# A hybrid attention and Hyena layer: bias tables assembled in DRAM, and the long convolutions without GpSimd

## The chip, the core and the metric

The kernel runs on one core of a Trainium2 chip. The metric is the device time of one execution in microseconds (us); lower is better. Below, PE is TensorE, DVE is VectorE, ACT is ScalarE, POOL is GpSimd and SP is SyncE, which here issues nearly all DMA transfers. "L841" is line 841 of the kernel before.

## What is computed

One layer over 1024 latent tokens (a grid of 16 rows by 64 columns) and 256 context tokens, model width 1024. After a modulated norm, one input projection feeds eight attention heads of 64 and a Hyena group of 512 channels. Both results are normed, put side by side and projected out; a gated ConvFFN (2816) follows. Cut to what the change touches:

```python
def _long_conv(u, k_f, bias):                      # FFT convolution, length 2L
    y = irfft(rfft(u, n=2*L) * k_f[None], n=2*L)[:, :L]
    return y + u * bias

def _hyena(hy, k_f, filt_bias):                    # two orders, one after the other
    x1, x2, v = jnp.split(hy, 3, axis=-1)
    z = x1 * _long_conv(v, k_f[:, 0], filt_bias[0])
    return x2 * _long_conv(z, k_f[:, 1], filt_bias[1])

def _neighbourhood_attention(q, k, v, k_ctx, v_ctx, rpb):
    # each latent query sees an 8 x 16 window of the grid (clipped at the edges) and all context keys
    bias = rpb[:, dr[:, None, :, None], dc[None, :, None, :]]
    s_loc = jnp.where(col_in, einsum(q, k_band) * scale + bias, NEG)    # NEG = -1e30
    s_ctx = einsum(q, k_ctx) * scale
    p = softmax(concatenate([s_loc, s_ctx]))
    ...
```

## The kernel before, in words

**Stage A** (to about 591 us): the norm, then 24 projections, each of 128 columns of the input weight over all 1280 tokens. A projection's weight arrives by one 512 KB DMA (`wr`, L606), is split into a high and a low part (`wh`, `wl`; three matmuls L116 to L118 replace one of full precision), with two buffers of each. The projections alternate between `qkv` and `hy_chunk`. `hy_chunk` (L652) applies the width-3 convolution on ACT and DVE into `cv` (two buffers), folds the result into the tile `fo` (POOL L663, L664, or ACT and DVE for one of three), transposes `fo` on PE and stores it to DRAM as `lxd` and `cxd`. **`fo` has one buffer.** Between the projections PE computes the implicit filters' spectra (matmuls into `psfA` and `psfB`), stored to DRAM as `Kd` and `Kc`. `rpb_frames` (L550) runs three times after the first group of projections. For each of three column variants it spreads the small bias table into frames, also in a tile with the tag `fo`, and stores them as `rpw` in DRAM (L558).

**Stage B** (about 437 to 915 us) has two strands. `chain(j)` (L770) computes the long convolutions, for four blocks of latent channels (j = 0 to 3) and once for the context (j = 4). Each call has two orders, here called *half-chains*, and each needs the one before it: forward DFT on PE (L802), twiddles (ACT L814 and L815, DVE L816), a butterfly over four residues (L823 to L828), the product with the filter's spectrum `K` (L841 to L844), an inverse butterfly (L849 to L854), twiddles (L858 to L860), inverse DFT on PE (L872), and a gate product (L877 to L885). The context's half-chains have no butterflies and no twiddles. The frequencies lie in two halves, h = 0 and 1; the butterflies and the product are written once for each half, dealt out between DVE and POOL. `K` has one buffer for each parity of j and comes in two loads of 512 KB, one for each half (L837). `attend(p_)` (L1001) handles a pair of heads, four times: scores (PE L1021), bias added and maximum taken on DVE (L1042), exponentials on ACT, transposes of the probabilities (PE L1065), products with the values (PE L979). Its bias comes in six tables `tb` of 128 x 736 numbers (two heads, three variants), which POOL fills once with NEG (L941); for each pair, 96 DMAs of 16 KB (L959) bring the rows of the frames into place.

**Stage C** (from about 915 us): group norms, output projection, ConvFFN, final norm.

The order of the work on each engine is fixed when the program is built, by a scheduler that runs the program through a model of the engines; `chain` is given high priority. On the chip each engine then runs its list strictly in order, and so does SP with its DMA issues; a DMA also waits for the one eight places ahead of it to be complete, because eight completion semaphores take turns.

The lines that the change and the prediction speak of:

Of the kernel before, what the change touches and what calls it, by code (L numbers as in the profile page):

```python
# [11 lines left out]
F32 = mybir.dt.float32  # L12
# [7 lines left out]
P = 128  # L20
# [3 lines left out]
LT = LL + LC  # L24
NH, DH = 8, 64
# [4 lines left out]
NEG = -1e30  # L30
# [44 lines left out]
HALF_ROWS = ((0, 11), (4, 12))  # L75
# [11 lines left out]
def _build(nc, tc, top, V, A, G, T, Q, I, O, dbg, upto):  # L87
# [458 lines left out]
    NROW = HALF_ROWS[0][1] + HALF_ROWS[1][1]  # L546
    HOFF = (0, HALF_ROWS[0][1] * 32)
    rpw = dr.tile([3, 16, NH, 4, 120], F32, name="rpw")

    def rpb_frames(t, var):  # L550
        f, g = t[:, 0:480], t[:, 512:992]
# [100 lines left out]
    def hy_chunk(which, j):  # L652

        cv = hyin((8, 0, 4)[which] + j)
        v = cv[:, 0:LL].rearrange("p (j r) -> p r j", r=4)
        lo, up = v[:, :, 0:128], v[:, :, 255:127:-1]
        clo, cup = cv[:, LL:LL + 128], cv[:, LL + 255:LL + 127:-1]
        fo = ip.tile([P, 2, 640], F32, tag="fo", name="fo", bufs=1)
        for i in range(2):
            d, dc = fo[:, i, 0:512].rearrange("p (r j) -> p r j", r=4), fo[:, i, 512:640]  # L660
            if which < 2:
                f = G.tensor_sub if i else G.tensor_add
                f(d, up, lo)  # L663
                f(dc, cup, clo)  # L664
            else:
                A.copy(d, up if i else lo)
                V.tensor_copy(dc, cup if i else clo)
        for i in range(2):
            ps = bk("tB")
            for r in range(4):  # L670
                T.transpose(ps[:, r * P:(r + 1) * P], fo[:, i, r * P:(r + 1) * P], ident)
            t = ip.tile([P, 512], F32, tag="st", name="st", bufs=2)
            A.copy(t, ps)
            Q.dma_start(out=lxd[j, which, :, i], in_=t)
        ps = bk("tB")
        for i in range(2):
            T.transpose(ps[:, i * P:(i + 1) * P], fo[:, i, 512:640], ident)
        t = ip.tile([P, 2, P], F32, tag="st", name="cx", bufs=2)
        A.copy(t, ps[:, 0:256].rearrange("p (i c) -> p i c", i=2))
        Q.dma_start(out=cxd[which, :, :, j * P:(j + 1) * P], in_=t)  # L680
# [56 lines left out]
    for j in range(4):  # L737
        for which in range(3):
            if j + which > 0:
                qkv(j, which)  # L740
            hy_chunk(which, j)
            if j + which == 0:

                t = ft([P, 512], "tm", bufs=2)
                e = "p a b -> p (a b)"
                Q.dma_start(out=t, in_=I["t_dft"].flatten().rearrange("(p x) -> p x", p=P))
                split(t, dft[0].rearrange(e), dft[1].rearrange(e))
                Q.dma_start(out=dlt, in_=I["t_delta"])
                Q.dma_start(out=nt, in_=I["t_nt"])
                with tc.issue_after(wloads[-1]):  # L750
                    Ws0 = w3load(0)
                filters(hs1, hs2, Ws0)
        cached(j)
        if j == 0:
            for var in range(3):
                rpb_frames(ip.tile([P, LT], F32, tag="fo", name="rp", bufs=1), var)
    fes.close()
    fbk.close()
    cbk = Banks("bkc", "right", "tile", cA=(1, 3))
# [10 lines left out]
    def chain(j):  # L770
# [21 lines left out]
        for o in range(2):  # L792
# [24 lines left out]
            if lat:  # L817
                ac = s4().rearrange(f4, h=2, i=2, q=2)
                X = s8()
                Xv = X.rearrange(f4, h=2, i=2, q=4)  # L820
                Xf = X.rearrange("p (h x c) -> p h x c", h=2, x=8)
                for h in range(2):
                    (G if h else V).tensor_add(ac[:, h], Gv[:, h, :, 0:2], Gv[:, h, :, 2:4])  # L823
                    V.tensor_sub(Gv[:, h, :, 2:4], Gv[:, h, :, 0:2], Gv[:, h, :, 2:4])
                    V.tensor_sub(Xf[:, h, 2:8:5], Gv[:, h, :, 2], Gv[:, h, ::-1, 3])
                    V.tensor_add(Xf[:, h, 3:7:3], Gv[:, h, :, 2], Gv[:, h, ::-1, 3])
                    V.tensor_add(Xv[:, h, :, 0], ac[:, h, :, 0], ac[:, h, :, 1])
                    (V if h else G).tensor_sub(Xv[:, h, :, 1], ac[:, h, :, 0], ac[:, h, :, 1])  # L828
                Y = Gt
            else:  # L830
                X = Gt
                Y = s8()
            Xs = X.rearrange("p (h i x) -> p h i x", h=2, i=2)
            Ys = Y.rearrange("p (h i x) -> p h i x", h=2, i=2)
            for h in range(2):
                Kt = cp.tile([P, 2, 512], F32, tag=f"K{b_}", name="K", bufs=1)
                Q.dma_start(out=Kt.rearrange(f1), in_=(Kd[o, j] if lat else Kc[o])[:, h * 1024:(h + 1) * 1024])  # L837
                kr = Kt[:, 0:1].to_broadcast([P, 2, 512])
                ki = Kt[:, 1:2].to_broadcast([P, 2, 512])
                B = s4().rearrange(v2, i=2)  # L840
                G.tensor_mul(B, Xs[:, h, ::-1], ki)  # L841
                V.tensor_mul(Ys[:, h], Xs[:, h], kr)
                V.tensor_sub(Ys[:, h, 0], Ys[:, h, 0], B[:, 0])
                V.tensor_add(Ys[:, h, 1], Ys[:, h, 1], B[:, 1])  # L844
            if lat:
                ac = s4().rearrange(f4, h=2, i=2, q=2)
                Gf = Gt.rearrange("p (h x c) -> p h x c", h=2, x=8)
                for h in range(2):
                    G.tensor_add(ac[:, h], Gv[:, h, :, 0:4:2], Gv[:, h, :, 1:4:2])  # L849
                    V.tensor_sub(Xv[:, h, :, 0:2], Gv[:, h, :, 0:4:2], Gv[:, h, :, 1:4:2])  # L850
                    V.tensor_add(Gf[:, h, 1:8:6], Xv[:, h, :, 0], Xv[:, h, ::-1, 1])
                    V.tensor_sub(Gf[:, h, 3:6:2], Xv[:, h, :, 0], Xv[:, h, ::-1, 1])
                    G.tensor_add(Gv[:, h, :, 0], ac[:, h, :, 0], ac[:, h, :, 1])
                    G.tensor_sub(Gv[:, h, :, 2], ac[:, h, :, 0], ac[:, h, :, 1])  # L854
                    for r in (1, 2, 3):
                        c, s, ns = tw_chain(h, r)
                        t = cp.tile([P, 2, P], F32, tag=f"t{b_}", name="t", bufs=TB)
                        A.activation(t[:, 0], Gv[:, h, 1, r], AF.Copy, scale=s)  # L858
                        A.activation(t[:, 1], Gv[:, h, 0, r], AF.Copy, scale=ns)
                        V.scalar_tensor_tensor(Gv[:, h, :, r], Gv[:, h, :, r], c, t, op0=ALU.mult, op1=ALU.add)  # L860
# [6 lines left out]
            for rp in range(2):  # L867
                pa = bk("cA")
                xs = slice(rp * 256, (rp + 1) * 256)
                for i in range(2):  # L870
                    for h in range(2):
                        T.matmul(pa[:, i * 256:(i + 1) * 256], idft[:, i, h], Ys[:, h, i, xs], start=h == 0,  # L872
                                 stop=h == 1, skip_group_check=True)
                pv = pa.rearrange(v2, i=2)
                tt = cp.tile([P, 2, 2, 256], F32, tag=f"s4{b_}", name="tt", bufs=S4B)
                if o == 0:
                    V.tensor_mul(tt[:, 0], pv, x1[:, :, xs])  # L877
                    V.tensor_mul(tt[:, 1], pv, x1[:, ::-1, xs])
                    G.tensor_add(un.rearrange(v2, i=2)[:, :, xs], tt[:, :, 0], tt[:, :, 1])
                else:  # L880
                    yt = tt[:, 0, 0]
                    A.copy(yt, pv[:, 0])
                    V.tensor_sub(ot[:, 0, xs], yt, pv[:, 1])
                    V.tensor_add(ot[:, 1, xs], yt, pv[:, 1])
                    G.tensor_mul(ot[:, :, xs], ot[:, :, xs], x2[:, :, xs])  # L885
            if o == 0:
                u = un
            elif lat:
# [47 lines left out]
        V.memset(t, 0.0)  # L936

    tbs = [[tp.tile([P, NROW * 32], F32, name=f"tb{h}{v}") for v in range(3)] for h in range(2)]
    for t in tbs:
        for v in t:  # L940
            G.memset(v, NEG)  # L941

    BLK = ((1, 4), (0, 4), (0, 4), (0, 3))
    Pring = [[tp.tile([P, 2, b - a, 16, 8], F32, name=f"Pl{h}{i}") for i, (a, b) in enumerate(BLK)] for h in range(2)]
    for r in Pring:
        for t in r:
            G.memset(t[:, 0, :, 11:16], 0.0)
            G.memset(t[:, 1, :, 0:4], 0.0)
    def bias_load(h, var):

        t = tbs[h % 2][var]
        for half in range(2):
            for rq in range(8):
                r = 8 * half + rq
                r0 = min(max(r - 4, 0), 8)
                nr = HALF_ROWS[half][1]
                a, d = r0 - HALF_ROWS[half][0], r0 - r + 7
                tv = t[rq * 16:(rq + 1) * 16, HOFF[half]:HOFF[half] + nr * 32].rearrange("q (u x) -> q u x", u=4)
                Q.dma_start(out=tv[:, :, a * 8:a * 8 + 64], in_=rpw[var, :, h, :, d * 8:d * 8 + 64])  # L959

    def stat(name, n=2):
        return tp.tile([P, n], F32, tag=name, name=name, bufs=4)

# [37 lines left out]
    def attend(p_):  # L1001
# [9 lines left out]
                        in_=I["cache_ctx_v"][0, 0, 2 * p_ + h].rearrange("(n p) d -> p n d", p=P))  # L1011
        for var in range(3):
            for h in range(2):
                bias_load(2 * p_ + h, var)
        kg = k[:, 0:LL].rearrange("p (u x) -> p u x", u=8)
        hs = [slice(h * DH, (h + 1) * DH) for h in range(2)]
        Pc = {}
# [639 lines left out]
    xs = {}  # L1657
# [107 lines left out]
```

## Time and profile before

| | us |
|---|---|
| median of three runs | 1921.23 (1920.3 to 1921.35) |
| the profiled execution, its own time | 1918.35 |
| its span in the trace | 1916.6 |
| PE, DVE, ACT, POOL busy | 1748.7, 1372.6, 885.0, 412.4 |
| first DFT matmul of the first half-chain | starts at 436.56 |
| first score matmul of the attention | starts at 628.91 |
| last subtraction and addition of the last half-chain | end at 912.03 |

Sums below are made against the profiled execution, 1918.35 us; the median of the runs is 2.9 us more. A row of the timeline reads: start in us, duration, engine, line, operation, output <- inputs, shapes, count, and in brackets how long the engine was idle before and what released it. A row of the windows reads: from:to, length, then busy time and instruction count of PE, PE's weight loads, DVE, ACT and POOL, then the granted TensorE clock, the DMA engines' busy share and GB/s.

### The profile page before, as it was taken

The page shows a single profiled execution, that of the slowest core. Times are in us where ns is not written, and L with a number is a line of the kernel's source. Part 1 is how long each engine was busy: PE and PEld are TensorE (multiplying, and loading weights), DVE is VectorE, ACT ScalarE, POOL GpSimd, SP SyncE. Part 2 cuts the span into 40 slices and gives each one's busy share as a digit, 9 for nine tenths or more (in the row PEclk, how much of TensorE's full clock was granted, in tenths as well). Part 3 has the DMA queues.
Part 4 walks back from the last instruction along what each step waited for, and adds up shares of the span by engine and source line. Part 5 has one row for each costly group of instructions (what it writes and reads, how often), then busy time and mean ns, then how long its engine had stood idle before and what let it go on. Part 6 is the DMA issues. An engine that isn't in the chain of part 4 may idle for free.

```text
span 1916.6 us, 27816 instructions
## 1 busy us (share of the span) xinstructions
PE 1748.7 (91%) x9999; PEld 1468.5 (77%) x9999; DVE 1372.6 (72%) x2175; ACT 885.0 (46%) x1827; POOL 412.4 (22%) x331
## 2 busy tenths in 40 slices
PE   5899989999994789789899699999999999999998
PEld 1688877887773345445688599999999999788786
DVE  4667648747777776776455888888877777656887
ACT  4654435434333355455555544444444444443352
POOL 2354546543654322233100000000000000000001
PEclk7999989999997799799899799999999999999999
DMA  7424444455433334421622154555322222853663
GB/s 266 133 75 129 130 128 119 143 170 170 139 111 122 84 96 94 108 63 56 209 99 100 57 161 163 164 168 173 114 72 73 72 62 71 286 184 109 207 209 127
DMA packets 238267, 249.80 MB, mean 130 GB/s; under 512 B 56610, under 2 KB 187795, under 8 KB 237873
## 3 DMA queue, kind: packets, MB, share of 16 engines
q1 hardware_dynamic: 236168, 247.09, 41.2%
q8 instruction: 79, 1.29, 0.3%
q10 hardware_dynamic: 1705, 0.82, 0.2%
q14 instruction: 59, 0.48, 0.1%
q0 software_dynamic: 256, 0.11, 0.0%
HBM read 176.75 MB, written 71.20 MB: 129 GB/s over the span
## 4 chain that ended last, share of the span: by engine, by line
PE 36%; DVE 10%; DMA 6%; issue 3%; ACT 3%; POOL 1%; SPq 0%; DVEq 0%; POOLq 0%; ACTq 0%
PE psd L118 6%; PE psd L116 6%; PE psd L117 6%; PE psa L116 2%; PE psa L117 2%; PE psa L118 2%; DMA wt<-in_w_down_dram 2%; DMA tdr<-wt 2%; PE psc L117 1%; PE psc L118 1%; PE psc L116 1%; PE psb L117 1%; PE psb L118 1%; PE psb L116 1%; DVE cv L1514 1%
## 5 line engine op out<-in xcount | busy, mean ns | idle before, releaser
L116 PE MATMUL psp<-hh,wh 128*128 128x512 f32 (+1 forms) x552 | 203.1, 368 | 2.3 <-ACT wh L121 1.9
L117 PE MATMUL psp<-hl,wh 128*128 128x512 f32 (+1 forms) x552 | 201.1, 364 | 0.0
L118 PE MATMUL psp<-hh,wl 128*128 128x512 f32 (+1 forms) x552 | 200.3, 363 | 0.0
L1680 POOL TENSOR_TENSOR rs<-rs,mhalf 128x1 f32<-128x1 f32 x10 | 7.7, 770 | 812.5 <-DVE rs L1679 812.5
L116 PE MATMUL psa<-T,ws 128*128 128x256 f32 (+1 forms) x528 | 166.1, 315 | 3.1 <-ACT rows L1480 3.0
L117 PE MATMUL psa<-T,ws 128*128 128x256 f32 (+1 forms) x528 | 165.6, 314 | 2.8 <-DVE T L1207 2.8
L118 PE MATMUL psa<-T,ws 128*128 128x256 f32 (+1 forms) x528 | 165.0, 313 | 0.0
L116 PE MATMUL psd<-wd,gs 128*128 128x512 f32 x360 | 140.5, 391 | 3.1 <-ACT gs L121 3.1
L117 PE MATMUL psd<-wd,gs 128*128 128x512 f32 x360 | 140.9, 391 | 0.0
L118 PE MATMUL psd<-wd,gs 128*128 128x512 f32 x360 | 124.9, 390 | 1.6 <-DVE gs L122 1.6
L116 PEld LDWEIGHTS psp<-hh,wh 128*128 128x128 f32 x552 | 106.5, 193 | 23.7 <-issue 7.0
L117 PEld LDWEIGHTS psp<-hl,wh 128*128 128x128 f32 x552 | 106.7, 193 | 15.0 <-issue 1.2
L116 PE MATMUL psc<-T,ws 128*128 128x384 f32 (+1 forms) x352 | 110.3, 313 | 8.4 <-ACT ws L121 8.4
L118 PEld LDWEIGHTS psp<-hh,wl 128*128 128x128 f32 x552 | 106.0, 192 | 14.9 <-issue 0.8
L117 PE MATMUL psc<-T,ws 128*128 128x384 f32 (+1 forms) x352 | 110.3, 313 | 0.0
L118 PE MATMUL psc<-T,ws 128*128 128x384 f32 (+1 forms) x352 | 110.1, 313 | 0.0
L117 PE MATMUL psb<-T,ws 128*128 128x384 f32 (+1 forms) x352 | 109.7, 312 | 0.0
L118 PE MATMUL psb<-T,ws 128*128 128x384 f32 (+1 forms) x352 | 109.6, 311 | 0.0
L116 PE MATMUL psb<-T,ws 128*128 128x384 f32 (+1 forms) x352 | 109.5, 311 | 0.0
L116 PEld LDWEIGHTS psa<-T,ws 128*128 128x128 f32 x528 | 101.4, 192 | 4.6 <-ACT rows L1480 4.5
L117 PEld LDWEIGHTS psa<-T,ws 128*128 128x128 f32 x528 | 101.5, 192 | 3.1 <-DVE T L1207 3.1
L118 PEld LDWEIGHTS psa<-T,ws 128*128 128x128 f32 x528 | 101.1, 192 | 0.0
(391 smaller groups left out, 4821.2 us busy)
## 6 DMA issues: line engine op xcount, KB each, us to landing
wada<-in_w_ada_dram SPq DMA_DIRECT2D x48, 512.0 KB
wr<-in_w_up_dram SPq DMA_DIRECT2D x44, 512.0 KB
gr<-gdr SPq DMA_DIRECT2D x44, 320.0 KB
wr<-in_w_in_dram SPq DMA_DIRECT2D x23, 512.0 KB
wt<-in_w_down_dram SPq DMA_DIRECT2D x44, 256.0 KB
tdr<-wt SPq DMA_DIRECT2D x44, 256.0 KB
gdr<-cv SPq DMA_DIRECT2D x22, 512.0 KB
wr<-tdr SPq DMA_DIRECT2D x20, 512.0 KB
```

What stands on the lines that cost most here:

```text
L116: T.matmul(out, ah, bh, start=start, stop=False, skip_group_check=True)
L117: T.matmul(out, ah, bl, start=False, stop=False, skip_group_check=True)
L118: T.matmul(out, al, bh, start=False, stop=stop, skip_group_check=True)
L1514: V.scalar_tensor_tensor(cv, r[:, 2:NC + 2], ffw(2, ch), cv, op0=ALU.mult, op1=ALU.add)
L1680: G.tensor_tensor(rs, rs, mhalf, op=ALU.pow)
```

## The change

It has two parts, and line numbers move by up to 28 (L606 becomes L626, L802 becomes L829, L841 becomes L867).

*Bias.* A new tensor `biasd` in DRAM holds the finished tables of all eight heads and three variants (24 tables of 376,832 bytes). After the frames, `bias_blank` takes the tile `fo`, fills it once with NEG on POOL (L554) and writes it 24 times (L556). Then `bias_rows`, called around `hy_chunk` for j = 1 and 2, copies the frames' rows over it, DRAM to DRAM: 192 DMAs of 32 KB, each 128 pieces of 256 bytes (L568). `attend` loads six whole tables with six DMAs. The 384 DMAs of L959 and the six fills of L941 go.

*Convolution.* Everything that POOL did in `chain` is done by DVE, and each butterfly operation covers both halves at once. The product with `K` is still done one half at a time, as are the inverse twiddles.

```diff
+    biasd = dr.tile([NH, 3, P, NROW * 32], F32, name="biasd")
+    def bias_blank(t, h):
+        if h == 0:
+            G.memset(t[:, 0:NROW * 32], NEG)
+        for var in range(3):
+            Q.dma_start(out=biasd[h, var], in_=t[:, 0:NROW * 32])
+    def bias_rows(var, half, rqs):
+        for rq in rqs:
...
+            for u in range(4):
+                Q.dma_start(out=tv[u, :, :, a * 8:a * 8 + 64], in_=rpw[var, :, :, u, d * 8:d * 8 + 64])
...
+            if j in (1, 2):
+                bias_rows(which, j - 1, range(4))
             hy_chunk(which, j)
+            if j in (1, 2):
+                bias_rows(which, j - 1, range(4, 8))
...
                 rpb_frames(ip.tile([P, LT], F32, tag="fo", name="rp", bufs=1), var)
+            t = ip.tile([P, LT], F32, tag="fo", name="rp", bufs=1)
+            for h in range(NH):
+                bias_blank(t, h)
...
-                for h in range(2):
-                    (G if h else V).tensor_add(ac[:, h], Gv[:, h, :, 0:2], Gv[:, h, :, 2:4])
-                    V.tensor_sub(Gv[:, h, :, 2:4], Gv[:, h, :, 0:2], Gv[:, h, :, 2:4])
...
+                V.tensor_add(ac, Gv[:, :, :, 0:2], Gv[:, :, :, 2:4])
+                V.tensor_sub(Gv[:, :, :, 2:4], Gv[:, :, :, 0:2], Gv[:, :, :, 2:4])
...
-                G.tensor_mul(B, Xs[:, h, ::-1], ki)
+                V.tensor_mul(B, Xs[:, h, ::-1], ki)
                 V.tensor_mul(Ys[:, h], Xs[:, h], kr)
...
-                    G.tensor_add(un.rearrange(v2, i=2)[:, :, xs], tt[:, :, 0], tt[:, :, 1])
+                    V.tensor_add(un.rearrange(v2, i=2)[:, :, xs], tt[:, :, 0], tt[:, :, 1])
...
-            bias_load(2 * p_ + h, var)
+            Q.dma_start(out=tbs[h][var], in_=biasd[2 * p_ + h, var])
```

The scheduler orders the changed program anew. Three places matter below.

**SP after the frames.** Before, the weight load L606 that follows the last frame's store stands fifteen rows behind it:

```order
L558 DMA rpw<-rp 128x480
L674 DMA lxd<-st 128x512 x2
L221 DMA wada_2_3543<-in_w_ada_dram 128x1024
L680 DMA cxd<-cx 256x1x128
...
L674 DMA lxd<-st 128x512
L680 DMA cxd<-cx 256x1x128
L606 DMA wr<-in_w_in_dram 128x8x128
```

Now the blanks follow the frames, and between them and the next weight load stand 128 row copies, with the first and the last of these rows:

```order
L578 DMA rpw<-rp 128x480
L556 DMA biasd<-rp 128x736 x16
L385 DMA fb<-in_filt_bias_dram 1x128
L556 DMA biasd<-rp 128x736 x8
...
L568 DMA biasd<-rpw 16x8x64 x16
L694 DMA lxd<-st 128x512
...
L221 DMA wada_1_4190<-in_w_ada_dram 128x1024
L568 DMA biasd<-rpw 16x8x64 x8
L694 DMA lxd<-st 128x512
L568 DMA biasd<-rpw 16x8x64
L694 DMA lxd<-st 128x512
L626 DMA wr<-in_w_in_dram 128x8x128
```

The weight load, the fifteenth of 24 loads on this row, has moved behind the copies and behind the stores of the projection just ahead of its own.

**POOL after the frames.** Before (`cs` is a filter's sum and difference):

```order
L557 COPY rp<-rp 128x15x4x8
L394 TENSOR_TENSOR cs_1825<-sd_1823,sd_1816 128x512
L395 TENSOR_TENSOR cs_1825<-sd_1823,sd_1816 128x512
L663 TENSOR_TENSOR fo<-cv 128x512
L664 TENSOR_TENSOR fo<-cv 128x128
```

Now:

```order
L577 COPY rp<-rp 128x15x4x8
L394 TENSOR_TENSOR cs_1826<-sd_1824,sd_1817 128x512
L395 TENSOR_TENSOR cs_1826<-sd_1824,sd_1817 128x512
L554 MEMSET rp 128x736
L394 TENSOR_TENSOR cs_1925<-sd_1918,sd_1911 128x512
...
L461 TENSOR_TENSOR cc<-cc,GO 128x512
L683 TENSOR_TENSOR fo<-cv 128x512
```

The next fold into `fo` has moved behind the fill with NEG and behind more of the filters' work.

**PE at the end of the attention.** Before, the context's half-chains (`dftf`, `idft`) lie among the attention's matmuls:

```order
L802 MATMUL pscA<-s_6396,dftf 128x256 x2
L979 MATMUL psav<-pt,vs 64x256 x2
...
L872 MATMUL pscA<-s_6432,idft 128x256 x4
L979 MATMUL psav<-pt,vs 64x256 x2
```

Now they stand in one block behind the attention's last row:

```order
L990 MATMUL psav<-pt,vs 64x256 x4
L1005 MATMUL psX<-lt,sel 128x128 x4
...
L898 MATMUL pscA<-s_6366,idft 128x256 x8
L829 MATMUL pscA<-s_6483,dftf 128x256 x8
L898 MATMUL pscA<-s_6502,idft 128x256 x8
L829 MATMUL pscA<-s_6519,dftf 128x256 x8
L898 MATMUL pscA<-s_6555,idft 128x256 x8
```

The last latent half-chain's inverse DFT and both context half-chains have moved behind all of the attention.

More of the change, by code (lines that the diff above doesn't have):

```diff
@@ L548, in _build @@
     rpw = dr.tile([3, 16, NH, 4, 120], F32, name="rpw")
+    biasd = dr.tile([NH, 3, P, NROW * 32], F32, name="biasd")
[6 more added lines that the diff above has]
+        for rq in rqs:
+            r = 8 * half + rq
+            r0 = min(max(r - 4, 0), 8)
+            nr = HALF_ROWS[half][1]
+            a, d = r0 - HALF_ROWS[half][0], r0 - r + 7
+            tv = biasd[:, var, rq * 16:(rq + 1) * 16, HOFF[half]:HOFF[half] + nr * 32].rearrange(
+                "h q (u x) -> u q h x", u=4)
+            for u in range(4):
+                Q.dma_start(out=tv[u, :, :, a * 8:a * 8 + 64], in_=rpw[var, :, :, u, d * 8:d * 8 + 64])
     def rpb_frames(t, var):
@@ L821, in chain @@
                 Xf = X.rearrange("p (h x c) -> p h x c", h=2, x=8)
-                for h in range(2):
-                    (G if h else V).tensor_add(ac[:, h], Gv[:, h, :, 0:2], Gv[:, h, :, 2:4])
-                    V.tensor_sub(Gv[:, h, :, 2:4], Gv[:, h, :, 0:2], Gv[:, h, :, 2:4])
[L825 to L828, printed above, removed]
+                V.tensor_add(ac, Gv[:, :, :, 0:2], Gv[:, :, :, 2:4])
+                V.tensor_sub(Gv[:, :, :, 2:4], Gv[:, :, :, 0:2], Gv[:, :, :, 2:4])
+                V.tensor_sub(Xf[:, :, 2:8:5], Gv[:, :, :, 2], Gv[:, :, ::-1, 3])
+                V.tensor_add(Xf[:, :, 3:7:3], Gv[:, :, :, 2], Gv[:, :, ::-1, 3])
+                V.tensor_add(Xv[:, :, :, 0], ac[:, :, :, 0], ac[:, :, :, 1])
+                V.tensor_sub(Xv[:, :, :, 1], ac[:, :, :, 0], ac[:, :, :, 1])
                 Y = Gt
@@ L847, in chain @@
                 Gf = Gt.rearrange("p (h x c) -> p h x c", h=2, x=8)
-                for h in range(2):
[L849 to L854, printed above, removed]
+                V.tensor_add(ac, Gv[:, :, :, 0:4:2], Gv[:, :, :, 1:4:2])
+                V.tensor_sub(Xv[:, :, :, 0:2], Gv[:, :, :, 0:4:2], Gv[:, :, :, 1:4:2])
+                V.tensor_add(Gf[:, :, 1:8:6], Xv[:, :, :, 0], Xv[:, :, ::-1, 1])
+                V.tensor_sub(Gf[:, :, 3:6:2], Xv[:, :, :, 0], Xv[:, :, ::-1, 1])
+                V.tensor_add(Gv[:, :, :, 0], ac[:, :, :, 0], ac[:, :, :, 1])
+                V.tensor_sub(Gv[:, :, :, 2], ac[:, :, :, 0], ac[:, :, :, 1])
+                for h in range(2):
                     for r in (1, 2, 3):
@@ L884, in chain @@
                     V.tensor_add(ot[:, 1, xs], yt, pv[:, 1])
-                    G.tensor_mul(ot[:, :, xs], ot[:, :, xs], x2[:, :, xs])
+                    V.tensor_mul(ot[:, :, xs], ot[:, :, xs], x2[:, :, xs])
             if o == 0:
@@ L938, in _build @@
     tbs = [[tp.tile([P, NROW * 32], F32, name=f"tb{h}{v}") for v in range(3)] for h in range(2)]
-    for t in tbs:
-        for v in t:
-            G.memset(v, NEG)
     BLK = ((1, 4), (0, 4), (0, 4), (0, 3))
@@ L948, in _build @@
             G.memset(t[:, 1, :, 0:4], 0.0)
[L949 to L959, printed above, removed]
     def stat(name, n=2):
```

## The prediction

> **What bounds the kernel now.** The page first: its engine totals and its slices, each slice 47.9 us long.
>
> ```profile
> PE 1748.7 (91%) x9999; PEld 1468.5 (77%) x9999; DVE 1372.6 (72%) x2175; ACT 885.0 (46%) x1827; POOL 412.4 (22%) x331
> PE   5899989999994789789899699999999999999998
> DVE  4667648747777776776455888888877777656887
> ```
>
> PE is nearly full except in the first slices and in slices 12 to 18, some 575 to 910 us. So the total says "PE", but what the change touches is a stretch in which PE waits. I read the windows there, cut at the ends of convolutions, with one short window of heavy transfers for a bandwidth:
>
> ```profile
> 289.00:437.00 148.00, 146.22 (x909) 122.23 (x910) 96.28 (x137) 65.28 (x141) 72.87 (x45) 1.00 0.51 154
> 437.00:629.00 192.00, 155.25 (x795) 123.24 (x793) 145.56 (x215) 67.40 (x162) 100.73 (x84) 0.88 0.41 125
> 629.00:858.00 229.00, 181.86 (x1011) 107.76 (x1011) 170.18 (x365) 118.62 (x389) 68.03 (x48) 0.87 0.37 90
> 858.00:912.00 54.00, 51.98 (x313) 31.59 (x314) 35.36 (x81) 28.94 (x90) 18.66 (x8) 1.00 0.20 60
> 420.00:432.00 12.00, 12.00 (x67) 9.04 (x67) 1.81 (x4) 2.68 (x4) 6.09 (x5) 1.00 0.94 314
> ```
>
> To 437 PE is full (146.2 of 148 us), and any hole made there is lost. From 437 the serial convolutions set the pace: PE is busy for 155 of 192 and 182 of 229 us. The timeline gives that line's marks:
>
> ```profile
> 436.56 0.81 PE L802 MATMUL pscA<-s,dftf 128*128 128x256 f32 x3
> 627.32 0.41 DVE L884 TENSOR_TENSOR s<-tt,pscA 128x256 f32<-128x256 f32 x1
> 628.91 0.49 PE L1021 MATMUL psS<-k,q 64*128 64x264 f32 x2
> 857.83 0.41 DVE L884 TENSOR_TENSOR s<-tt,pscA 128x256 f32<-128x256 f32 x1
> 911.62 0.41 DVE L884 TENSOR_TENSOR s<-tt,pscA 128x256 f32<-128x256 f32 x1
> 913.41 0.37 SPq L893 DMA_DIRECT2D hyd<-s  x1
> ```
>
> Four half-chains take 436.6 to 627.7 (191 us), four more to 858.2 with most of the attention beside them, the context's two to 912.0 (54 us), and the output projection follows the store at 913.4. My sum is the shift of this end: the start of the first half-chain, four half-chains, four beside the attention, two of the context. What comes after is unchanged, and shifts whole.
>
> **The start: `fo`, the queue, the order.** The next fold into `fo` ran at once after the frames, and the next weight loads looked like this:
>
> ```profile
> 280.83 2.13 POOL L663 TENSOR_TENSOR fo<-cv 128x512 f32<-128x512 f32 x1
> 273.29 0.40 SPq L606 DMA_DIRECT2D wr<-in_w_in_dram  x1
> 323.86 0.38 SPq L606 DMA_DIRECT2D wr<-in_w_in_dram  x1
> 379.11 1.05 ACT L121 CAST wh<-wr 128x1024 fp32r<-128x1024 f32 x1 [0.42 <-PE psp L117]
> ```
>
> *Term 1, the blanks.* 24 x 376,832 bytes are 9.04 MB out of the one `fo`. The window at 420 moved 314 GB/s at a busy share of 0.94, so 334 GB/s with the engines full: 27 us, from about 281 to 308, in which no projection of the Hyena group gets past `cv`. The scheduler has filled in 62 more filter matmuls; at 148 us for 909 (first window) they are 10 us that need not be done later. Net **+17**. Bounds: +5 if the two `cv` buffers and three PSUM banks let PE run on; +40 if other transfers, 154 GB/s in the first window, take their part of the 334 and leave 180 (50 us).
>
> *Term 2, SP.* The fifteenth weight load was issued at 323.9, long before its projection began, near 379, when the projection two ahead had left the buffer. Now it is queued behind 128 copies, and, as the order shows, behind the stores of the fourteenth projection's own `fo`. The nearest rows for an issue are the old table loads and, for many small pieces, the frames' loads:
>
> ```profile
> L959 SPq DMA_DIRECT2D tb<-rpw x384: 302/424/1596, 612.1 to 835.6; - x192
> L556 SPq DMA_DIRECT2D rp<-in_rpb_dram x48: 653/667/1402, 200.1 to 272.5; - x48
> 612.10 16.18 SPq L959 DMA_DIRECT2D tb<-rpw  x30
> ```
>
> Thirty in a row took 16.18 us, 0.54 each: I take this, since it has the same source and pieces of the same size. 128 copies are 69 us, and the 47 other issues between them at about 0.4 (the load's row) are 19: from the last blanks, near 300, the queue is free near 390 if nothing in it waits. But the fourteenth projection, which ran to about 388 before, now ends near 405, and its result still goes through DVE, POOL (2.13 for the fold), PE, ACT and the store before the load is even issued, near 416; the load then needs some 4 us (a load of `K` of the same 512 KB takes 3.75, below), the split 1.05 and POOL's part about 2.4. PE would be ready for the fifteenth near 411, where the new order puts it 86 instructions (14 us) later than the old one; it gets it near 425. **+14**; +0 if copies and stores run earlier and the other rows of PE cover it, +31 if each copy takes 0.67.
>
> *Term 3, the order.* Up to the first DFT, PE's list now has about 70 more instructions than before; at 0.163 each **+11** (0 to 15). The first half-chain thus starts near 479, 42 us late.
>
> **The half-chains.** These rows give DVE's durations beside a busy POOL, and alone:
>
> ```profile
> L841 POOL TENSOR_TENSOR s<-s,K x20: 2347/3327/3458, 445.5 to 900.8; 128x1024 f32<-128x1024 f32 x20
> 445.70 3.28 DVE L842 TENSOR_TENSOR s<-s,K 128x1024 f32<-128x1024 f32 x1
> 873.14 1.23 DVE L842 TENSOR_TENSOR s<-s,K 128x1024 f32<-128x1024 f32 x1 [0.63 <-DMA K<-Kc]
> 876.62 0.69 DVE L843 TENSOR_TENSOR s<-s,s 128x512 f32<-128x512 f32 x1 [0.70 <-POOL s L841]
> 896.87 3.75 DMA K<-Kc
> ```
>
> The same product takes DVE 3.28 us in one place and 1.23 in another; POOL needs 3.3 for its share, and DVE then waits for it. On DVE alone 1024 columns cost 1.23, 512 cost 0.69, 256 cost 0.41 (L884 above). So moving POOL's work to DVE costs DVE little: half a product is 1.23 + 1.23 + 0.69 + 0.69 = 3.84 us, where POOL alone needed 3.3 before the two sums could follow. Merged butterflies are two operations of 1024 and four of 512, 2 x 1.23 + 4 x 0.69 = 5.2. But merging also makes each half wait for the other: no butterfly starts before all six twiddles are done. The twiddles are paced by ACT and DVE in turn:
>
> ```profile
> 439.14 0.48 DVE L816 SCALAR_TENSOR_TENSOR s<-pscA,tw,t 128x256 f32<-128x256 f32 x1
> 471.81 0.48 DVE L860 SCALAR_TENSOR_TENSOR s<-s,tw,t 128x256 f32<-128x256 f32 x1 [0.43 <-ACT t L859]
> 473.19 0.48 DVE L860 SCALAR_TENSOR_TENSOR s<-s,tw,t 128x256 f32<-128x256 f32 x1 [0.89 <-ACT t L859]
> 474.44 0.49 DVE L860 SCALAR_TENSOR_TENSOR s<-s,tw,t 128x256 f32<-128x256 f32 x1 [0.76 <-ACT t L859]
> 479.82 0.68 DVE L878 TENSOR_TENSOR tt<-pscA,s 128x512 f32<-128x512 f32 x1
> ```
>
> One per 1.3 us. A half-chain is then: DFT and six twiddles 2.6 + 5 x 1.4 + 0.5 = 10; butterfly 5.2; first product's multiplications 2.46, then the reload of the one `K` buffer 3.75 (its own sums hidden under it), then the second half 3.84, together 10.1; butterfly 5.2; six twiddles 7.8; inverse DFT and gate (474.9 to 480.5) 5.6. Sum 44 us, four of them 176 against 191: **term 4, -15**. Bounds: 41 each (-27) with twiddles at 1.0, and 48 each (0) if DVE's other work cuts in as now.
>
> **Term 5, attention beside four half-chains.** All of the attention now precedes the context block; before, a good part lay beside it. The PE group rows from 858 to 915 tell the context's share:
>
> ```profile
> L802 PE MATMUL pscA<-s,dftf 128*128 128x256 f32 x32 | 8.7, 396 | 0.0
> L872 PE MATMUL pscA<-s,idft 128*128 128x256 f32 x32 | 8.0, 383 | 0.0
> ```
>
> Of the 1011 + 313 matmuls of the last two windows, 64 are the context's; the other 1260 must now fit beside four half-chains. The two windows give two rates: 4.4 matmuls per us (1011 in 229) where latent half-chains ran beside, and 5.8 (313 in 54) where PE was 96% busy. At the one 1260 take 286 us, at the other 217. I take the middle rate, 5.1: the slow window holds the start of the attention with its waits for data, but DVE (170 of 229 us busy) gets POOL's share on top, with the contention gone. That is 247 against 229: **+18**. Bounds: 5.6 and 4.75 per us, 225 and 265. The end of the small table loads is worth little, since DVE waited for tables 8.9 us in six places, and the attention starts, as before, behind four half-chains in PE's list:
>
> ```profile
> DVE Pl L1042 <- DMA tb<-rpw: 8.9, 6, 2.5
> ```
>
> **Term 6, the context's half-chains.** Without butterflies and twiddles, each is DFT and copies 4 + product 10.1 + inverse DFT and gate 5.6 + 1 for steps from engine to engine = 21, so 42 against 54: **-12** (-14 to -8). They run faster, but now with PE empty: the price of that lies in term 5.
>
> The sum: 17 + 14 + 11 - 15 + 18 - 12 = **+33**, 1918.35 + 33 = 1951, and with the 2.9 us up to the median **1954**.
>
> **Rivals.** *The convolutions win (faster).* One mechanism: DVE's contention with POOL is the whole pace of the line, so that without POOL the half-chains fall to 41 and the attention beside them stays at 229 (5.5 matmuls per us). With copies issued at 0.42 (median of L959's row) term 2 vanishes: 17 + 0 + 11 - 27 + 0 - 14 = -13, a median of **1908**. For it speak the 3.28 against 1.23; against it, that the twiddle steps, which POOL has no part in, are 40% of a half-chain, and that PE was full before 437. It decides if the first DFT starts before about 467 and four half-chains take under 165 us.
>
> *The small pieces cost more (slower still).* Copies from DRAM to DRAM in 256-byte pieces appear nowhere in the trace; the row with the most pieces per byte is L556, 0.67. At that rate the 128 copies take 17 us more, and the 64 between the next five weight loads about 10 more: +60, **1981**. The Trainium skill, "DMA: Bandwidth & Descriptors", section Specifications, speaks against the change here: a piece under 512 bytes falls short of line rate, as the engine must read, merge and write. No run here yet shows that for DRAM as a target; the table loads, of 256-byte pieces into SBUF at 0.54, neither bear it out nor exclude it.
>
> *Nothing measurable.* The line's gain and the late start cancel: copies at 0.42 (term 2 at 0), half-chains at 42 (-23), the attention at 236 (+7), the context as in the sum: 17 + 0 + 11 - 23 + 7 - 12 = 0, **1921**.
>
> **How the numbers follow.** The forecast's case 0.52, the faster rival 0.28, the slower 0.14, no change 0.06. A difference under 0.2% (3.8 us) is one that a measurement of this kernel can't tell. So faster 0.28, same 0.06, slower 0.66. Alone, the forecast's case reaches from 1933 to 1970; the range that holds 8 in 10 must take in most of both other cases: 1900 to 1988.
>
> **What would show it.** Right: POOL's first fold after the frames near 308 instead of 281; the weight load near 416 with PE idle before it; the first DFT near 479; DVE products at 1.23 throughout, half-chains of 44 us; a hole in PE of some 40 us before the output projection. Wrong: a first DFT before 467 (terms 1 to 3), half-chains near 48 or 41 (term 4), context half-chains ending near the attention's end (terms 5 and 6).

## The result: 3.7% slower, and two losses behind it

The changed kernel takes 1991.52 us (median of 4 runs, 1989.3 to 1993.84) against 1921.29 us: a ratio of 1.0365, 95% interval 1.0347 to 1.0383. Forecast was 1954, so the direction held and the size did not: +70 us where +33 were summed up. The profiled execution of the changed kernel took 1990.65 us, 72.3 more than that of the kernel before.

### The profile after

The page of the changed kernel, its engine totals and slices (49.7 us each):

```profile
PE 1757.1 (88%) x9999; PEld 1473.0 (74%) x9999; DVE 1364.7 (69%) x2183; ACT 885.8 (45%) x1827; POOL 246.8 (12%) x222
PE   6899977939997398787589879999999999999998
PEclk7999978969998799898689989999999999999999
```

POOL lost 166 us of work and DVE, which took most of it over, gained none in sum: its own operations became shorter (the last section shows which). PE has new holes, in slices 5 to 8 and at 18 to 19 (counted from 0). The windows of the changed kernel, cut at the same marks as before (first DFT, end of the fourth, the eighth and the tenth half-chain; columns as before):

```profile
289.00:503.00 214.00, 167.84 (x961) 138.81 (x962) 90.93 (x142) 69.66 (x149) 73.03 (x48) 0.85 0.61 174
503.00:686.00 183.00, 142.90 (x750) 113.51 (x749) 133.20 (x213) 64.24 (x156) 28.47 (x30) 0.88 0.48 149
686.00:943.00 257.00, 211.80 (x1283) 126.58 (x1281) 194.51 (x425) 145.31 (x473) 0.00 (x0) 0.94 0.23 75
943.00:988.00 45.00, 25.00 (x64) 15.12 (x64) 22.04 (x30) 5.43 (x10) 0.00 (x0) 0.70 0.23 70
```

The first stretch, which PE filled before (146.2 of 148 us), now has 46 us of waits in it, and the last one has the context alone on the chip: 64 matmuls in 45 us. The marks themselves, read from the timelines of both kernels as in the prediction:

| stretch | before | after | forecast |
|---|---|---|---|
| first DFT starts at | 436.6 | 503.4 (+67) | +42 |
| four half-chains | 191.2 | 181.9 (-9) | -15 |
| four beside the attention | 230.5 | 258.1 (+28) | +18 |
| the context's two | 53.8 | 44.4 (-9) | -12 |
| store of the context's result | 913.4 | 988.5 (+75) | +33 |

More than half of the miss is in the first row. SP's own rows there, the first blanks, the first and the last long row of copies ahead of the weight load, the load itself, and the group of all copies (ns: least, median, largest):

```profile
283.07 13.14 SPq L556 DMA_DIRECT2D biasd<-rp  x16
309.70 10.51 SPq L568 DMA_DIRECT2D biasd<-rpw  x16
432.86 5.00 SPq L568 DMA_DIRECT2D biasd<-rpw  x8
440.91 0.43 SPq L626 DMA_DIRECT2D wr<-in_w_in_dram  x1
L568 SPq DMA_DIRECT2D biasd<-rpw x192: 511/597/1742, 309.7 to 492.6; - x192
```

The weight load came at 440.9, not near 416. SP's list itself was the limit: from 309.7 to 440.9 it issued 128 copies in 85 us (0.66 each) and 65 other DMAs in 34 us, and stood idle for some 12. What PE waited for, from its timeline and from its waits between 270 and 503 (sum in us, times, longest):

```profile
417.93 0.45 PE L752 MATMUL pstB<-ident,ck 128*128 128x128 f32 x1 [7.25 <-DMA ck<-in_cache_ctx_k_dram]
431.13 0.65 PE L225 MATMUL pstB<-wada,silc 128*32 128x256 f32 x4 [10.28 <-DMA wada<-in_w_ada_dram]
436.56 0.65 PE L225 MATMUL pstB<-wada,silc 128*32 128x256 f32 x4 [4.35 <-DMA wada<-in_w_ada_dram]
447.90 0.80 PE L116 MATMUL psp<-hh,wh 128*128 128x512 f32 x1 [7.79 <-ACT wh L121]
PE pstB L225 <- DMA wada<-in_w_ada_dram: 16.9, 3, 10.3
```

Not the weight load, but other loads behind the copies stopped PE first: the cached keys `ck` (L752) and the modulation weights `wada` (L225). In PE's list these stand ahead of the transposes of the fourteenth projection's `fo`, whose store stands ahead of the weight load in SP's list. So the copies delay PE by way of other loads before they delay it by way of the weights. These four waits are 30 us. The way back, from PE to SP, was short: SP waited 1.5 us for that store.

A wait costs more than its length. From 420 to 440 PE was busy for 5.18 of 20 us, and its granted clock stood at 0.50:

```profile
420.00:440.00 20.00, 5.18 (x28) 2.61 (x28) 1.10 (x4) 0.96 (x2) 0.31 (x1) 0.50 0.69 194
460.00:480.00 20.00, 20.00 (x117) 17.01 (x116) 4.25 (x9) 4.62 (x8) 6.78 (x3) 1.00 0.45 110
```

The Trainium skill, "TensorE: Matmul & The Clock Gate", Part 1, says the clock is halved unless PE has been busy lately; this trace agrees (0.50 beside 1.00).

### The profile page after: what moved, and what is told of

Same layout as the page of the kernel before. It is cut to its first block, busy times and chain, and to the rows that moved or that the text cites. A ratio compares the mean times of both kernels' runs of the same rounds, so it can differ in the third digit from the quotient of the medians.

```text
span 1988.9 us, 27327 instructions
## 1 busy us (share of the span) xinstructions
PE 1757.1 (88%) x9999; PEld 1473.0 (74%) x9999; DVE 1364.7 (69%) x2183; ACT 885.8 (45%) x1827; POOL 246.8 (12%) x222
## 4 chain that ended last, share of the span: by engine, by line
PE 59%; DVE 16%; DMA 10%; ACT 6%; issue 5%; SPq 2%; POOL 2%; POOLq 0%; DVEq 0%; ACTq 0%
PE psd L116 6%; PE psd L118 6%; PE psd L117 6%; PE psp L116 4%; PE psp L118 4%; PE psp L117 4%; PE psa L116 2%; PE psa L117 2%; PE psa L118 2%; PE pscA L898 2%; DMA wt<-in_w_down_dram 2%; PE psc L116 2%; PE psc L117 2%; PE psc L118 2%; PE psb L117 2%
## 5 line engine op out<-in xcount | busy, mean ns | idle before, releaser
L898 PE MATMUL pscA<-s,idft 128*128 128x256 f32 x160 | 58.6, 513 | 54.4 <-DVE s L886 39.9
L116 PEld LDWEIGHTS psa<-T,ws 128*128 128x128 f32 x528 | 101.2, 192 | 4.1 <-ACT rows L1491 3.9
L117 PEld LDWEIGHTS psa<-T,ws 128*128 128x128 f32 x528 | 101.2, 192 | 3.1 <-DVE T L1218 3.1
```

What stands on the lines that cost most here:

```text
L116: T.matmul(out, ah, bh, start=start, stop=False, skip_group_check=True)
L117: T.matmul(out, ah, bl, start=False, stop=False, skip_group_check=True)
```

## Experiments

Two theories were set against each other to begin with. **Q**: the loss is the late start, made by the number of copies in SP's queue. **C**: the convolutions without POOL are a gain, and the new tables lengthen the attention. The first four runs do one part alone, take the copies out, and move them. All runs below fall into three groups, and the kernel before, run again beside each, had medians of 1921.4, 1920.6 and 1918.4 us; ratios are against these, and differences between runs of different groups are good to some 3 us.

**The convolutions alone.** The function `chain` of the changed kernel, in the kernel before.

```diff
-    (chain as before: halves one at a time, shared by DVE and POOL)
+    (chain as changed: halves merged, all on DVE)
     bias_load(2 * p_ + h, var)   # 384 small loads, as before
```

> The convolutions as in the change, the bias tables as before. Theory Q (the loss is the late start, made by the copies in SP's queue): the first DFT stays near 437; the four half-chains take 183 us as in the changed kernel (191 before), the four beside the attention 257 (230 before), the context's two 45 (54 before), in sum +10, a time near 1931. Rival C (the convolutions without POOL are a gain, and the longer stretch beside the attention comes from the new bias tables): the stretch beside the attention stays near 230, and the time is near 1905.

1952.83 us, 1.0162 (1.0140 to 1.0185). The first DFT is at 435.7 and four half-chains take 184.2, as Q had it; the stretch beside the attention takes 280.0, more than either theory said (257 and 230), and so the time is 22 us over Q's. What waits there, between 590 and 900:

```profile
DVE s L840 <- DMA K<-Kd: 38.3, 5, 10.8
PE psav L978 <- DVE pt L968: 26.1, 7, 12.4
```

The product with `K`, now on DVE, waits for a load of `K` that stands among the small table loads; DVE's list is in order, so the attention's copies `pt` wait behind it, and PE behind those. In the kernel before, neither DVE nor POOL waits for one of these loads (from 430 to 1000 us their only waits for `K` are 7 us for the context's). A later run below has the same small loads, all of POOL's work on DVE and the halves apart, and there DVE waits 0.5 us for them. So it is the merging, with the order that comes with it, and not POOL's work on DVE. C falls for this part: the convolutions' half of the change is a loss by itself, of 31 us.

**The bias tables alone.** The function `chain` of the kernel before, in the changed kernel.

> The bias tables as in the change, the convolutions as before, with POOL. Q: the first DFT near 503 as in the changed kernel, then 191 + 230 + 54 us as before, a time near 1987. C: the same late start, but a stretch beside the attention of 257, a time near 2014.

1966.81 us, 1.0235 (1.0216 to 1.0254). The first DFT is at 500.4: the late start belongs to the tables. But the rest is better than both theories said, 182.5 + 223.2 + 54.2. The new tables save 7 us in the attention, and the half-chains, which start late, have fewer projections beside them (that this is what makes them shorter was not tried by itself; the next run bears on it). The two parts alone cost 45 and 31 us, 77 together; both at once cost 70.

**No copies.**

```diff
-            for u in range(4):
+            for u in range(0):
                 Q.dma_start(out=tv[u, ...], in_=rpw[...])
```

> The changed kernel without the 192 row copies (the tables stay blank, so the bias of the window is left out); the blanks are still written out of the one fold buffer. Q: PE no longer waits behind SP (30 us of waits near 410 to 450 go), the first DFT comes near 437 + 17 (the blanks) less what the new order puts ahead, 430 to 455, the time near 1925 to 1945. Rival B (the blanks are most of the loss): the first DFT stays later than 480, the time over 1965.

The loop runs no times, so this kernel leaves the window's bias out of its result. It takes 1926.63 us, 1.0025 (1.0016 to 1.0035): 65 us less than the changed kernel. The first DFT comes at 428.2. B falls: the blanks are not most of it. Their price shows in the window from 281 to 320, here and in the kernel before:

```profile
281.00:320.00 39.00, 27.59 (x139) 24.58 (x139) 29.75 (x43) 21.18 (x54) 22.78 (x18) 0.68 0.73 273
281.00:320.00 39.00, 36.36 (x233) 30.63 (x232) 29.92 (x44) 23.19 (x58) 26.03 (x17) 0.96 0.36 106
```

94 matmuls fewer, 15 us at the 0.163 of the prediction, against 17 there. That the first DFT still comes early is the order: 2227 matmuls run ahead of it where the kernel before has 2374, 147 fewer, 24 us, and 436.6 + 15 - 24 = 427.6.

The start is 75 us earlier than in the changed kernel and the time only 65 us less, because four half-chains take 197.1 us here and 181.9 there, with the same `chain`. The kernels with the halves apart, below, go the same way: 168.7 from a start at 433.9, 165.6 from 463.4, 157.8 from 499.9. So part of a late start comes back in shorter half-chains. One run stands against it, the convolutions alone (184.2 from 435.7), and the reason was not tried.

**Copies issued by POOL.**

```diff
-                Q.dma_start(out=tv[u, ...], in_=rpw[...])
+                G.dma_start(out=tv[u, ...], in_=rpw[...])
```

> The changed kernel with the 192 copies issued by POOL, whose work in the convolutions is gone, in place of SP. Q: SP's loads come on time, the first DFT near 430 to 450, the context's half-chains lie among the attention again, a time of 1910 to 1940. Rival D (the small pieces themselves load the DMA engines and hold up the other transfers, whichever engine issues them): weight loads still land late, the first DFT after 480, a time over 1965.

1974.24 us, 1.0274 (1.0249 to 1.0298). D's time came out, and not by D's cause. The first DFT is at 475.8, a little before D's 480; the group of copies, POOL's busy time up to there (fifth sum of the window), and PE's longest wait in it:

```profile
L568 POOL DMA_DIRECT2D biasd<-rpw x192: 531/531/629, 305.9 to 526.1; - x192
281.00:476.00 195.00, 140.99 (x777) 117.83 (x777) 96.31 (x136) 66.92 (x148) 146.24 (x205) 0.81 0.56 167
PE psp L118 <- POOL wl L122: 13.4, 1, 13.4
```

A copy takes 0.53 us of POOL's list, and POOL's own work, the split of the weights (L122) and the filters' sums, stands behind the copies. Of PE's waits in this window only 8 us are for DMAs. The queue moved to another engine, and with it the wait.

**Fewer copies.** If the number of issues is the cause, the same bytes in a quarter of the issues must be cheaper. With head and quarter side by side in the tables, one copy takes all four quarters (the blanks become six DMAs, and each pair's tables come in twelve):

```diff
+    biasd = [dr.tile([3, P, NH, HALF_ROWS[i][1] * 32], F32, ...) for i in range(2)]
...
-            for u in range(4):
-                Q.dma_start(out=tv[u, :, :, a * 8:a * 8 + 64], in_=rpw[var, :, :, u, d * 8:d * 8 + 64])
+            tv = biasd[half][var, rq * 16:(rq + 1) * 16].rearrange("q h (u x) -> q (h u) x", u=4)
+            Q.dma_start(out=tv[:, :, a * 8:a * 8 + 64],
+                        in_=rpw[var].rearrange("q h u x -> q (h u) x")[:, :, d * 8:d * 8 + 64])
```

> The changed kernel with the finished tables laid out as row, head, quarter, so that one copy takes all four quarters: 48 copies of 128 KB (512 pieces of 256 bytes each) in place of 192 of 32 KB, the same bytes in the same pieces; the blanks are six DMAs, and each pair loads its tables with 12 DMAs in place of 6. Theory Q (the number of issues decides, about 0.6 us of SP each): the weight loads come on time, the first DFT near 440, then as in the changed kernel, a time near 1934. Rival E (the pieces decide): each copy takes about 2.4 us of SP, the first DFT stays near 500, the time near 1990.

> The 48 copies of the run before, with the convolutions as before the change, POOL included. Q: the first DFT near 440, 191 us for four half-chains, 277 for the attention's stretch with the context as in the run of the bias tables alone: a time of 1910 to 1922, at or a little under the kernel before. E: near 1966.

With the changed convolutions 1958.31 us, 1.0195 (1.0176 to 1.0214); with those of before 1925.16, 1.0027 (1.0018 to 1.0037). Q had 1934 and 1910 to 1922, E 1990 and 1966. Against their counterparts with 192 copies, 33 and 42 us less. The group of 48 copies:

```profile
L566 SPq DMA_DIRECT2D biasd<-rpw x48: 469/624/4427, 295.9 to 342.8; - x48
```

512 pieces take SP 0.62 us in the median, 128 took 0.60. In sum the 48 copies take SP 39 us, where 192 at 0.66 would take 127: for these copies the issue is paid, far more than the piece, and E falls. The first DFT came at 460.0 and 463.7, later than Q's 440. The window from 281 to 320 has only 106 matmuls here, 127 fewer than before (21 us): the blanks still hold `fo`, and the copies run in between at full DMA load. So the tables without their queue cost little and win nothing: 1925 is still 4.6 us over the kernel before, beside which it ran.

The second question is why the convolutions' half lost. **M1**: POOL's work in DVE's list. **M2**: the merging of the halves, through the order that it makes the scheduler choose.

**Not merged, all on DVE.**

```diff
-                V.tensor_add(ac, Gv[:, :, :, 0:2], Gv[:, :, :, 2:4])
+                for h in range(2):
+                    V.tensor_add(ac[:, h], Gv[:, h, :, 0:2], Gv[:, h, :, 2:4])
...
```

and so for the other eleven butterfly operations.

> The changed kernel with each butterfly done one half at a time, all on DVE. The stretch from the end of the fourth half-chain to the end of the last was 284 us before, 302 in the changed kernel, 277 with the bias part alone. Theory M1 (POOL's work in DVE's list stretches it): near 300 or more, a time of 1988 or more. Rival M2 (the merging stretches it, by making the scheduler put the context's half-chains behind all of the attention; here they lie among it again): 277 to 287, a time of 1965 to 1975.

1939.67 us, 1.0106 (1.0085 to 1.0126): **52 us less than the changed kernel**, with the same tables and nearly the same late start (499.9). Four half-chains take 157.8 instead of 181.9, and the stretch to the end takes 278.5 instead of 302.5. M1 falls. M2 has that stretch right, and the context lies among the attention again, but the time is 25 us under its range: that the four half-chains ahead of the attention would shorten by 24 us, neither theory had, and the place of the context has no part in them. Against the bias part alone, which differs only in that POOL shares the work, it is 27 us less. So taking POOL out of the chain is a gain, and merging turned it into a loss. The first half-chain in DVE's timeline, of the changed kernel first:

```profile
511.32 0.48 DVE L843 SCALAR_TENSOR_TENSOR s<-pscA,tw,t 128x256 f32<-128x256 f32 x1 [1.76 <-ACT t L842]
512.78 0.47 DVE L843 SCALAR_TENSOR_TENSOR s<-pscA,tw,t 128x256 f32<-128x256 f32 x1
513.83 1.21 DVE L849 TENSOR_TENSOR s<-s 128x1024 f32<-128x1024 f32 x1
521.66 1.21 DVE L867 TENSOR_TENSOR s<-s,K 128x1024 f32<-128x1024 f32 x1
529.33 1.23 DVE L867 TENSOR_TENSOR s<-s,K 128x1024 f32<-128x1024 f32 x1 [3.52 <-DMA K<-Kd]
539.94 0.48 DVE L886 SCALAR_TENSOR_TENSOR s<-s,tw,t 128x256 f32<-128x256 f32 x1
```

and with the halves apart (its lines are one or two higher from L849 on):

```profile
505.59 0.48 DVE L843 SCALAR_TENSOR_TENSOR s<-pscA,tw,t 128x256 f32<-128x256 f32 x1
506.59 0.42 DVE L854 TENSOR_TENSOR s<-s 128x256 f32<-128x256 f32 x1
508.32 1.21 DVE L868 TENSOR_TENSOR s<-s,K 128x1024 f32<-128x1024 f32 x1
511.38 0.47 DVE L843 SCALAR_TENSOR_TENSOR s<-pscA,tw,t 128x256 f32<-128x256 f32 x1
520.37 1.23 DVE L868 TENSOR_TENSOR s<-s,K 128x1024 f32<-128x1024 f32 x1
527.00 0.47 DVE L887 SCALAR_TENSOR_TENSOR s<-s,tw,t 128x256 f32<-128x256 f32 x1
```

Apart, the first half's butterfly runs in the gaps between the second half's twiddles (the row at 506.59), its product starts 6.4 us after the first twiddle (501.89), and the reload of `K` is issued at 511.5, long before DVE wants it (520.4). Merged, DVE sits idle between twiddles (0.7 to 1.8 us, four times), the first product starts 16.3 us after the first twiddle (505.34), and DVE waits 3.52 us for the second load of `K`, which was issued at 524.0, when the first product had read the buffer. Over the latent half-chains DVE waits 13.5 us for `K` merged, and not at all apart.

**One multiplication back on POOL.**

```diff
-                V.tensor_mul(B, Xs[:, h, ::-1], ki)
+                G.tensor_mul(B, Xs[:, h, ::-1], ki)
```

> The changed kernel with one of the product's two multiplications (128 x 1024, twenty of them) back on POOL, all butterflies merged on DVE. M1: the stretch falls to 285 to 292, as DVE is rid of 25 us of work, a time of 1973 to 1981. M2: the context still stands behind most of the attention, the stretch stays at 298 or more, a time of 1987 or more.

1993.65 us, 1.0377 (1.0359 to 1.0396), the stretch 301.2: nothing gained by relieving DVE, as M2 had it. The run is weak evidence by itself, since the multiplication takes POOL 2.3 to 3.5 us where DVE takes 1.2, and it stands in the serial chain.

**One of the two mergings.** For the forward one alone, the butterfly ahead of the product stays merged and that behind it is taken apart as above; for the inverse one alone, the other way round.

> The changed kernel with the forward butterflies merged and the inverse ones one half at a time. The merging of both cost 52 us. Theory J1 (the forward merging costs more: the first half's product and its load of the spectrum wait for all six twiddles): 1970 or more. Rival J2 (the inverse merging costs more: the first half's inverse butterfly and twiddles wait for the reload of the one buffer of the spectrum and the second product): 1950 to 1964. As the scheduler again puts the context behind the attention here, some 7 us of the difference stay in any case.

> The changed kernel with the inverse butterflies merged and the forward ones one half at a time. J1: 1950 to 1964. J2: 1970 or more.

1975.33 us, 1.0296 (1.0280 to 1.0312), and 1950.35 us, 1.0173 (1.0149 to 1.0195). The forward merging costs 36 us and the inverse one 11, against the run with neither. Some of that gap is the order, since the context stands behind the attention in the first of the two runs and partly beside it in the second. The four half-chains ahead of the attention are free of that: 179.4 and 161.5, against 157.8 with neither and 181.9 with both. J1 is right: what hurts most is that the first product, and with it the reload of `K`, wait for all six twiddles.

How much of it is the order? In the run with copies on POOL, the butterflies were merged but the context's half-chains lay among the attention's matmuls again. There the stretch took 295.9, against 302.5 with the context at the end and 278.5 unmerged. So some 7 of those 24 us can be the order (that run differs in its start too), and the other 17 would be the merged half-chains themselves. The 24 us of the first four half-chains come on top.

**The better version.** What remains is a kernel with the old tables, or the 48 copies, and the halves apart on DVE.

> The bias tables as before the change; the convolutions without POOL, each butterfly one half at a time on DVE. Theory M2 (POOL's removal is a gain, the merging lost it): the first DFT near 436, four half-chains near 160 us (158 in the run with new tables), then 278 to 305 for the stretch with the attention (the upper end if DVE waits for the filter's spectrum behind the 384 small table loads as it did in the merged run, 30 us): a time of 1883 to 1913, under the kernel before. Rival M1 (POOL's work on DVE costs, and the gain in the run before came from the new tables): 1925 or more.

> The bias tables by 48 copies, and the convolutions without POOL one half at a time. M2: the first DFT near 460 as in the other runs of 48 copies, 158 and 275 after it, a time near 1900, under the kernel before. M1: 1925 or more.

1902.65 us, **0.9920 (0.9903 to 0.9937)**, and 1908.53 us, 0.9950 (0.9934 to 0.9965): both a little faster than the kernel before, by 0.8% and 0.5%, the one that leaves the tables alone more so. Its windows:

```profile
289.00:434.00 145.00, 144.28 (x899) 120.72 (x898) 95.00 (x136) 61.95 (x133) 71.70 (x44) 1.00 0.51 156
434.00:603.00 169.00, 145.73 (x792) 117.20 (x791) 139.90 (x263) 66.23 (x162) 34.51 (x36) 0.93 0.47 142
603.00:846.00 243.00, 186.41 (x1034) 111.01 (x1032) 180.43 (x424) 121.97 (x401) 0.00 (x0) 0.86 0.35 85
846.00:899.00 53.00, 50.26 (x316) 31.96 (x314) 38.52 (x79) 28.52 (x85) 0.00 (x0) 1.00 0.21 61
```

PE is full again up to the first DFT, four half-chains take 169 us instead of 191 (near 160 was expected), and some of that is given back: the stretch beside the attention takes 243 instead of 230, since the attention now comes earlier than its small table loads. Its waits between 590 and 900:

```profile
DVE Pl L1042 <- DMA tb<-rpw: 20.7, 8, 6.4
PE psS L1021 <- DMA tb<-rpw: 9.8, 1, 9.8
```

Here whole tables would help, if their preparation were free; with 48 copies the stretch is 220, but the start 30 us later.

## Why the prediction was wrong, step by step

**Term 1, the blanks (+17): right.** The fold came at 308.9 (308 forecast), and the loss in that window is 15 us.

**Term 2, SP (+14): mis-sized, and the largest error.** By difference it is some 45 us: 67 of late start, less 15 for the blanks and 7 for the order. The prediction had SP's list free near 390, and so made the fourteenth projection's store, near 416, what the weight load waits for. That step failed. SP's list itself was the limit, and the load came at 440.9. The copies began at 309.7, not near 300; 128 of them took 85 us, not 69 (the pace was 0.66, not 0.54); 65 other DMAs took 34 us, not 47 of them 19; and some 12 us were idle, 1.5 of them for that store. Besides, the step "PE, ACT and the store" was costed as work that runs when its inputs are there, while PE's list has rows ahead of those transposes which wait for loads behind the same copies (L752 and L225): 22 us of waits that no term held. With the wait for the weights itself that is 30, and the slow clock comes on top: from 281 to the first DFT, PE was busy 174.5 us for 1004 matmuls, 0.174 each, against 152.1 for 948 before, 0.160.

**Term 3, the order (+11): near.** The traces count 2420 matmuls up to the first DFT, 46 more than before (70 were taken), 7 us.

**Term 4, four half-chains (-15): right in kind.** 45.5 us each instead of the 44 worked out, 181.9 in sum. But the sum was then compared with a kernel in which POOL shares the work, and so hid that two changes of opposite sign are in it: POOL out, -25, and merging, +24 (157.8 unmerged, 182.5 with POOL, all with the new tables and a late start; with the old tables and a start on time, -22 and +16). The prediction named the cost, "merging also makes each half wait for the other", and never asked what the half-chain would be without it. One reading under it was wrong as well: of the two rows given as "beside a busy POOL, and alone", the short one at 873.14 also ran beside a POOL product (see the last section).

**Term 5, beside the attention (+18): +28.** The rate was 5.0 matmuls per us (1283 in 257), where 5.1 was taken. That all of the attention would come ahead of the context was read rightly from the order. Why it is slow is not what was said: DVE is no fuller than before (194.5 of 257 us, against 170.2 of 229), it is the merged half-chain that is long: with the halves apart, this stretch and the context's together take 278.5 us in place of 302.5, some 7 of which can be the order.

**Term 6, the context (-12): -9.** 22 us each instead of 21.

**The rivals.** The faster one, that POOL's contention is the pace of the half-chains, was right that POOL in the chain costs time: without POOL and without merging, four of them take 157.8, under the 165 it named. But that is from a start at 499.9; from a start on time they take 168.7. It needed the start on time and the halves apart, and the change had neither. How much of the gain is contention, and how much that POOL is slower at the same work, the runs do not separate. The one of the small pieces is refuted in its cause: a copy of 512 pieces is issued in the time of one with 128. That short pieces move fewer bytes for the same load of the DMA engines does show: with 48 copies, the window from 320 to 360 moved 204 GB/s at a busy share of 0.90, where the large loads of the prediction's window moved 314 at 0.94. But PE was busy all of that window, so it did not set the time there. For the time it was nearest, 1981, since its pace of 0.67 came out (0.66).

## What to carry to other kernels

A DMA costs the list that issues it time of its own, here about 0.6 us for a copy of 128 pieces as for one of 512 (other DMAs took from 0.2 us for a small load to 2.7 in the median for the six large blanks). Many small ones are to be judged by what is queued behind them, in every list that waits for that queue, and here a layout that lets one DMA do the work of four was worth more than another queue. Merging two halves of a pipeline into one operation saves instructions and takes away the overlap of one half's waits with the other's work; on this serial chain that was the dearer side. When a change has two parts, each needs its own sum against a kernel without it, or a gain and a loss of like size will pass for nothing.

## What was not expected of the hardware

The same DVE product takes 1.22 us in each of twenty places in the changed kernel; twenty before had a median of 1.76 and took up to 3.28, beside POOL.

```profile
L868 DVE TENSOR_TENSOR s<-s,K x20: 1212/1218/1220, 522.8 to 976.5; 128x1024 f32<-128x1024 f32 x20
L842 DVE TENSOR_TENSOR s<-s,K x20: 1224/1760/3284, 445.7 to 900.7; 128x1024 f32<-128x1024 f32 x20
445.51 2.39 POOL L841 TENSOR_TENSOR s<-s,K 128x1024 f32<-128x1024 f32 x1 [1.09 <-issue]
873.17 3.42 POOL L841 TENSOR_TENSOR s<-s,K 128x1024 f32<-128x1024 f32 x1 [4.16 <-ACT s L805]
```

It is not enough that POOL is busy: ten of the twenty took 1.22 or 1.23 while POOL's own product ran beside them. What counts is which starts first. POOL's product at 445.51 started before DVE's (445.70) and took 2.39; DVE's took 3.28 and ended 1.1 us after it. At 873.14 DVE started first and took 1.23, and POOL's took 3.42. In all twenty places the one that starts second ends as if it had begun when the first was done. The Trainium skill, "GPSIMD Engine Reference", Specifications, has VectorE and GpSimd share an interface to SBUF, with contention when a VectorE operation has two SBUF inputs; these rows agree.

What it adds up to shows in the pair with the new tables that differs only in POOL's share: DVE's busy time went from 1365.0 to 1367.9 us while it took over the work that makes up most of POOL's fall from 402.5 to 247.3. The size of the gain in the whole time, 16 to 27 us (the pairs with the old tables, with 48 and with 192 copies), was more than the prediction's sums gave it. And moving a copy from SP to POOL saves little of the list that issues it: 0.53 us on POOL, 0.60 on SP, both with 128 pieces.
